# First tile of the combined projection: modulation weights split into a scale half and a shift half, the shift half loaded and used later

## The chip, the cores and the metric

One core of a Trainium2 chip. The metric is the device time of one execution in microseconds (us); the number given for a kernel is the median of several runs. Five engines work side by side from their own queues of instructions: TensorE (PE; PEld is its weight load), VectorE (DVE), ScalarE (ACT), GpSimd (POOL) and SyncE (SP), which here issues nearly all DMAs. SBUF is the on-chip memory of 128 partitions, PSUM the accumulator with 8 banks of 512 fp32 columns.

## The reference

One layer of a diffusion backbone over 512 latent tokens and 256 context tokens of width 1024. What matters for the change is its beginning:

```
mod = silu(c) @ w_mod + b_mod                    # 6 x 1024 columns; the same for c_ctx
sh1, sc1, gt1, sh2, sc2, gt2 = split(mod, 6)
h_lat = rmsnorm(x, norm1_g) * (1 + sc1) + sh1    # h_ctx likewise from ctx, c_ctx
p_lat = h_lat @ w_in                             # one projection, its columns feed everything after
```

Behind it come a bidirectional state-space mixer, a windowed attention, two gates, an output projection, and a gated convolutional feed-forward stage with a final norm. Everything is fp32.

## The kernel before, in words

Activations lie transposed, channels on the partitions: the 1024 channels are eight tiles of 128, and a tile of the latents is 128 x 512. Products that need fp32 accuracy are made of three passes with operands split in a high and a low part: high times high, high times low, low times high.

The opening stage (the block under `with tc.tile_pool(name="spool"`, lines 304 to 540) computes the modulation, the normed input and, at the same time, the first five column blocks of the projection (the gates g 0 to 4). So as to start before the norm is known, the first four tiles (`NU = 4`) are multiplied by the scale only (`scaled`, L410), their products are scaled by the norm afterwards (`scale_banks`), and the shift enters through a small product of its own (`shifts`, L427). For each tile j there are these steps, named by a letter in the string `order` (L518):

- A (`mod_rows`, L367): 8 products (16 PE instructions at L374, fp32 in two passes) of silu(c) with two loads of modulation weights, 2j and 2j + 1; each load holds half of the input channels and, for them, 128 shift columns and 128 scale columns of the tile. Four groups of 32 partitions of the bank `pmod` collect the sums in columns 0 to 255. ScalarE copies them out (L376), and the tile's projection weights `w0_raw[j]` are split (L149 and L150; the first tile on VectorE, L153 and L154). From tile 3 on, A also issues the load of the next tile's w0.
- B (`mod_cols`, L382): two products (four instructions, L384) turn the rows into columns, into `pmod` columns 256 to 259; ScalarE makes of them the scale `a1` (L385, from 258 and 259) and the shift `s1` (L386, from 256 and 257). Below these two are called a(j) and s(j).
- H (`prep`): `ah` and `al`, the high and the low part of x times the scale (L413 on ScalarE, L414 on VectorE), for the later tiles the normed input itself.
- P (`products`, L417): P0:02 is tile 0 on the output blocks 0 and 1, three passes (L422), and so on.
- Z (`shifts`, L427, L431): the shift times the raw w0 into the bank `pbias`, for the first four tiles.

sq_0 to sq_3 sum the squares of x (L397 on ScalarE, L399 on VectorE), sum_l (L241, then `ms` on VectorE, L251, and a power on GpSimd) and put_l make the norm of them; `hold` and `keep` are filler products on a bank that nobody reads.

What sets the order: PE runs exactly in the order of the string (`tc.manual_schedule`). SP's queue holds the loads in the order in which they are written (lines 331 to 347, then those that the steps issue), each with a wait when its buffer isn't free yet; modulation weights share six buffers, w0 four. ScalarE's and VectorE's queues are put in order when the kernel is built, by the builder's own view of what is ready; the copies of L376 and the squares of L397 are pinned behind what stands ahead of them in the text on their engine (`keep_in_program_order`). The waits between engines are put in by the builder too.

The order of the loads before: cc, modulation weights 0 and 1, the identity, a part of the vectors, w0 of tile 0, x tile 0, weights 2 and 3, w0 1, x tile 1, weights 4 and 5, w0 2, then x in three loads of two tiles, weights 6 and 7, w0 3, the other vectors. A load of modulation weights or of two x tiles has 512 KB, one of w0 320 KB, one of an x tile 256 KB.

Of the kernel before, what the change touches and what calls it, by code (L numbers as in the profile page):

```python
# [9 lines left out]
F32 = mybir.dt.float32  # L10
F32R = mybir.dt.float32r
U8 = mybir.dt.uint8
AF = mybir.ActivationFunctionType
# [5 lines left out]
P = 128  # L19
# [3 lines left out]
KT = D // P  # L23
# [4 lines left out]
V_BMOD = 0  # L28
V_N1 = 48
# [15 lines left out]
def tile_hybrid_layer(  # L45
# [33 lines left out]
    V, S, G, T = nc.vector, nc.scalar, nc.gpsimd, nc.tensor  # L79
# [221 lines left out]
    NU, NG = 4, 5  # L301
    first = {}
    gates = []
    with tc.tile_pool(name="spool", bufs=1) as sp:
        xs_ = sp.tile([P, KT, L], F32, name="xsb")
        xc_ = sp.tile([P, KT, LC], F32, name="xcb")
        csil32 = sp.tile([P, KT, 32], F32, name="csil32")
        s32 = sp.tile([P, KT, 32], F32, name="s32")
        s1 = s32[:, :, 0:2]
        still = sp.tile([P, 256], F32R, name="still")  # L310
        sel2 = sp.tile([P, 2], F32, name="sel2")
# [3 lines left out]
        def load_mod(i):  # L315
            t = sp.tile([P, 4, 256], F32, tag="wm", name="wm", bufs=6)
            nc.sync.dma_start(t, wm1[i].rearrange("p (k c) -> p k c", k=4))
            return t

        def load_w0(j):  # L320
            r = sp.tile([P, 640], F32, tag="w0", name="w0", bufs=4)
            nc.sync.dma_start(r, w0[j])
            return r

        def load_x(k):
            nc.sync.dma_start(xs_[:, 2 * k : 2 * k + 2, :], xT[k].rearrange("p (k t) -> p k t", k=2))
# [2 lines left out]
            nc.sync.dma_start(xs_[:, k, :], xT[k // 2, :, k % 2 * L : k % 2 * L + L])  # L329

        nc.sync.dma_start(ccs, cc)
        mod_raw = {i: load_mod(i) for i in range(2)}
        nc.sync.dma_start(ident, ident_d)
        nc.sync.dma_start(vec[:, :V_N2], vecs[:, :V_N2])
        w0_raw = {0: load_w0(0)}
# [4 lines left out]
        mod_raw.update({i: load_mod(i) for i in (4, 5)})  # L340
        w0_raw[2] = load_w0(2)
        load_x(1)
        load_x(2)
        load_x(3)
        mod_raw.update({i: load_mod(i) for i in (6, 7)})
        w0_raw[3] = load_w0(3)
        nc.sync.dma_start(vec[:, V_N2:], vecs[:, V_N2:])
        G.memset(raw(still), 1.0)
        G.memset(csil32, 0.0)
# [14 lines left out]
        pmod, pbias = accb(), accb()  # L364
        pg = [misb() for _ in range(NG)]

        def mod_rows(j):  # L367

            for u in range(2):
                i = 2 * j + u  # L370
                w = mod_raw.pop(i) if i in mod_raw else load_mod(i)
                for k in range(4):
                    z = slice(32 * k, 32 * k + 32)
                    T.matmul(pmod[z, 0:256], csil32[:, 4 * u + k, :], w[:, k, :], start=u == 0, stop=u == 1)  # L374
            row = tmp("tm")[:, :256]
            tc.keep_in_program_order(S.copy(row, pmod[:, 0:256]))  # L376
            if j + 1 < KT and j + 1 not in w0_raw:
                w0_raw[j + 1] = load_w0(j + 1)
            W[j] = split_w(j)
            return row  # L380

        def mod_cols(j, row):  # L382
            for i in range(2):
# [33 lines left out]
        def products(j, w, h, gs=range(NG)):  # L417

            st, en = j == 0, j in (NU - 1, KT - 1)
            for a, b in ((0, 0), (0, 1), (1, 0)):  # L420
                for i in gs:
                    T.matmul(  # L422
                        pg[i], w[a][:, i * P : (i + 1) * P], h[b], start=st and a + b == 0, stop=en and a == 1,
                        skip_group_check=True,
                    )

        def shifts(j):  # L427

            for g in range(3):
                n = 256 if g < 2 else P  # L430
                T.matmul(  # L431
                    pbias[32 * g : 32 * g + 32, 0:n], s32[:, j, :], w0_raw[j][:, 256 * g : 256 * g + n],
                    start=j == 0, stop=j == NU - 1,
                )

        r, W, H = {}, {}, {}
# [16 lines left out]
        def hold(n):  # L453
            for _ in range(n):
                T.matmul(unread[:, :256], still[:, :P], still, start=True, stop=True)
# [21 lines left out]
        def load_next():  # L477
# [9 lines left out]
        rows = {}  # L487
# [10 lines left out]
            "sq_2": lambda: squares(xs_, ssq, L, range(2, 4)),  # L498
            "sq_3": lambda: squares(xs_, ssq, L, range(4, 8)),
            "hold": lambda: hold(18),  # L500
            "keep": lambda: hold(6),
            "sq_c": lambda: squares(xc_, cq, LC, range(4)),
            "sq_d": lambda: squares(xc_, cq, LC, range(4, 8)),
            "sum_l": lambda: sums("l", ssq, 4),
# [11 lines left out]


        order = """  # L518
            hold A0 keep B0 H0 sq_0 keep Z0 P0:02 A1 P0:23 B1 H1 sq_1 P0:35 A2 P1:02 B2 H2 sq_2 P1:25 Z1 P2:02 sq_3 A3 P2:23 B3 H3
            P2:35 sum_l Z2 P3:02 A4 put_l P3:23 B4 H4 P3:35 scale_a Z3 scale_b rows A5 half P4:02 B5 H5 cols P4:25 A6  # L520
            P5:02 B6 H6 P5:24 A7 ctx N0 P5:45 B7 H7 next P6:02 N1 P6:25 N2 P7:02 sq_c N3 P7:25 sq_d
        """
        with tc.manual_schedule(engines={mybir.EngineType.PE}):
# [1563 lines left out]
def pack(  # L2087
    x, c, ctx, c_ctx, w_mod, b_mod, norm1_g, norm2_g, w_in, ssd_conv_w, ssd_conv_b, ssd_dt_bias, ssd_a_log, ssd_d,
    ssd_norm_g, w_o_ssd, w_o_att, att_sink, w_out, w_up, ffn_conv_w, ffn_conv_b, w_down, final_g,
):  # L2090
    f = lambda a: np.asarray(a)
    x, c, ctx, c_ctx, w_mod, w_in = f(x), f(c), f(ctx), f(c_ctx), f(w_mod)[0], f(w_in)[0]
    w_o_ssd, w_o_att, w_out, w_up, w_down = f(w_o_ssd)[0], f(w_o_att)[0], f(w_out)[0], f(w_up)[0], f(w_down)[0]
    ca = np.ascontiguousarray
    z0, xbc0, dt0 = 0, 2048, 5120
    q0 = dt0 + 64
    k0, v0, g0 = q0 + 1024, q0 + 1280, q0 + 1536
    half = np.r_[0:16, 32:48, 16:32, 48:64]
    perm = lambda base, heads: np.concatenate([base + 64 * h + half for h in range(heads)])
    A = np.arange  # L2100
    d = {}
    d["xT"] = ca(x[0].T.reshape(4, 2, P, L).transpose(0, 2, 1, 3).reshape(4, P, 2 * L))
    d["ctxT"] = ca(ctx[0].T.reshape(2, 4, P, LC).transpose(0, 2, 1, 3).reshape(2, P, 4 * LC))
    d["cc"] = ca(np.stack([c[0], c_ctx], 1).reshape(KT, P, 2).transpose(1, 0, 2))
    cw, fw = f(ssd_conv_w)[0], f(ffn_conv_w)[0]
    d["vecs"] = ca(
        np.concatenate(
            [_per_channel(f(a)) for a in (b_mod[0], norm1_g[0], norm2_g[0], final_g, ssd_norm_g[0])]
            + [_per_channel(cw[i]) for i in range(3)]
            + [_per_channel(f(ssd_conv_b)[0])]  # L2110
            + [_per_channel(fw[i]) for i in range(3)]
            + [_per_channel(f(ffn_conv_b)[0])],
            axis=1,
        )
    )
    dta = np.stack([f(ssd_dt_bias)[0].reshape(64), f(ssd_a_log)[0].reshape(64)], 1).reshape(2, 1, 32, 2)
    d["dta"] = ca(np.repeat(dta, 2, axis=1).reshape(P, 2))
    d["bc"] = ca(np.concatenate([f(ssd_d)[0], f(att_sink)[0]]))
    d["wm1"] = ca(w_mod[:, :2048].reshape(2, 4, P, 2, KT, P).transpose(4, 0, 2, 1, 3, 5).reshape(16, P, 1024))
    d["wm2"] = ca(w_mod[:, 2048:].reshape(4, 2, P, 8, 512).transpose(3, 0, 2, 1, 4).reshape(8, 4, P, 1024))  # L2120
    d["wq"] = _cols(w_in, perm(q0, 16))
    d["wk"] = _cols(w_in, perm(k0, 4))
    vdt = ca(w_in[:, np.r_[v0:g0, dt0:q0]].reshape(KT, P, 320).transpose(1, 0, 2)).reshape(P, KT * 320)
    d["wv"] = ca(np.pad(vdt, ((0, 0), (0, 320))).reshape(P, 3, 960).transpose(1, 0, 2))
    d["w0"] = ca(w_in[:, g0 : g0 + 640].reshape(KT, P, 640))
    d["wx"] = _cols(w_in, A(xbc0, dt0))
    d["wz"] = _cols(w_in, A(z0, xbc0))
    d["wg"] = _cols(w_in, A(g0, g0 + 2048))
    d["woa"] = _cols(w_o_att, A(1024))
    d["wos"] = _cols(w_o_ssd, A(1024))  # L2130
    d["wout"] = _cols(w_out, A(1024))
# [30 lines left out]
```

## Time and profile before

| | us |
|---|---|
| median of 3 runs | 1232.68 (1231.74 to 1234.01) |
| the profiled execution | 1232.22 |
| its span, first to last instruction | 1230.4 |
| PE busy | 1218.5 (99%) |
| VectorE busy | 914.1 (74%) |
| ScalarE busy | 687.0 (56%) |

A row of the timeline gives the start and the length of an instruction (or of several merged ones, xN), its engine, line and operation, out<-in, and in brackets how long the engine was idle ahead of it and what ended that. Matmuls are pipelined: a row of two has the length to the end of the second, and the next row can start before it ends. A row of the view by stretches gives start and end, then for PE, PEld, DVE, ACT and POOL the busy time and the number of instructions, then TensorE's granted clock, the share of the DMA engines' time that was used, and GB/s. A row of the DMA issues gives the transfer, its size and the time from issue to landing; where such a row is shown, it is of a window that holds that one issue. Buffers of `wm1` are called wm, those of `w0` w, those of x xsb.

### The profile page before, as it was taken

To read this page: it belongs to the slowest core of one execution; us is meant where nothing else is said; L and a number is where in the kernel's file an instruction comes from. 1 tells how busy PE (TensorE), PEld (TensorE's weight loads), DVE (VectorE), ACT (ScalarE), POOL (GpSimd) and SP (SyncE) were. 2 spreads that over 40 slices of the span, in tenths; PEclk is the share of its full clock that TensorE was granted. 3 is DMA by queue.
4 is the path that set the end of the run, shared out by engine and by line. 5 is a ranking of instruction groups with operands and counts; after the bars stand their busy time and mean duration, and the time that the engine had idled before them with its cause. 6 is when DMAs were issued, how large, how long until landed. Compare 5 with 4: busy or idle time off the path is not lost.

```text
span 1230.4 us, 17460 instructions
## 1 busy us (share of the span) xinstructions
PE 1218.5 (99%) x6328; PEld 996.3 (81%) x6328; DVE 914.1 (74%) x1484; ACT 687.0 (56%) x1302; POOL 167.9 (14%) x174
## 2 busy tenths in 40 slices
PE   9999999999999999999999999999999999999997
PEld 6798888888878877777777778888988888888886
DVE  4757888888555698697886786677688788886566
ACT  4657787787443556566586572223544444444543
POOL 0000111121100033333351530000200000000000
PEclk9999999999999999999999999999999999999999
DMA  9652678877946235345347466776144444457785
GB/s 354 245 159 89 218 194 194 212 198 211 225 141 211 91 123 147 121 131 185 122 138 203 136 205 221 225 245 236 48 166 148 145 150 153 153 169 248 243 318 183
DMA packets 108630, 224.65 MB, mean 183 GB/s; under 512 B 9600, under 2 KB 48832, under 8 KB 108544
## 3 DMA queue, kind: packets, MB, share of 16 engines
q1 hardware_dynamic: 101056, 197.32, 48.9%
q0 software_dynamic: 6912, 25.17, 8.7%
q8 instruction: 50, 0.82, 0.3%
q10 hardware_dynamic: 576, 1.05, 0.2%
q14 instruction: 36, 0.29, 0.1%
HBM read 193.29 MB, written 49.87 MB: 198 GB/s over the span
## 4 chain that ended last, share of the span: by engine, by line
PE 92%; DVE 3%; DMA 2%; ACT 2%; issue 1%; SPq 0%; POOLq 0%; ACTq 0%; DVEq 0%
PE acc L197 19%; PE acc L200 19%; PE acc L198 19%; PE acc L1919 3%; PE acc L1917 3%; PE acc L1918 3%; PE score L811 3%; PE po L860 3%; PE pt L847 2%; PE mis L1480 2%; PE mis L1385 2%; DMA wm<-wm 1%; PE mis L422 1%; PE acc L930 1%; PE acc L931 1%; PE acc L932 1%
## 5 line engine op out<-in xcount | busy, mean ns | idle before, releaser
L197 PE MATMUL acc<-hlh,whi 128*128 128x512 f32 x488 | 199.3, 408 | 0.0
L150 DVE TENSOR_TENSOR wlo<-wraw,whi 128x1024 fp32r<-128x1024 f32 (+2 forms) x119 | 143.4, 1207 | 71.9 <-ACT whi L149 62.2
L149 ACT CAST whi<-wraw 128x1024 fp32r<-128x1024 f32 (+2 forms) x119 | 122.8, 1033 | 127.4 <-PE acc L198 75.0
L200 PE MATMUL acc<-hlh,wlo 128*128 128x512 f32 x488 | 191.4, 392 | 0.0
L198 PE MATMUL acc<-hll,whi 128*128 128x512 f32 x488 | 190.7, 391 | 0.0
L197 PE MATMUL acc<-mh,whi 128*128 128x512 f32 x360 | 141.0, 392 | 0.0
L200 PE MATMUL acc<-mh,wlo 128*128 128x512 f32 x360 | 140.1, 389 | 0.0
L198 PE MATMUL acc<-ml,whi 128*128 128x512 f32 x360 | 140.0, 389 | 0.0
L200 PEld LDWEIGHTS acc<-hlh,wlo 128*128 128x128 f32 x488 | 91.6, 188 | 20.3
L198 PEld LDWEIGHTS acc<-hll,whi 128*128 128x128 f32 x488 | 91.9, 188 | 17.5 <-issue 1.7
L197 PEld LDWEIGHTS acc<-hlh,whi 128*128 128x128 f32 x488 | 91.8, 188 | 17.5 <-issue 2.2
L198 PEld LDWEIGHTS acc<-ml,whi 128*128 128x128 f32 x360 | 67.6, 188 | 14.5 <-issue 0.5
L197 PEld LDWEIGHTS acc<-mh,whi 128*128 128x128 f32 x360 | 67.6, 188 | 14.3 <-issue 0.5
L200 PEld LDWEIGHTS acc<-mh,wlo 128*128 128x128 f32 x360 | 67.6, 188 | 14.2
L820 DVE CUSTOM_DVE_ANT_0 p<-score,winm,nsink 128x512 f32<-128x512 f32 (+1 forms) x64 | 51.9, 810 | 15.2 <-PE score L811 13.7
L1268 DVE SCALAR_TENSOR_TENSOR ta<-acc,half,ta 128x511 f32<-128x511 f32 (+1 forms) x66 | 43.8, 663 | 25.7 <-ACT ta L1267 25.6
L1267 ACT ACTIVATE ta<-acc,half 128x512 f32<-128x512 f32 (+1 forms) x66 | 46.7, 708 | 27.0 <-PE acc L200 25.7
L1275 ACT ACTIVATE tb<-ta 128x512 f32<-128x512 f32 (+1 forms) x44 | 23.5, 534 | 65.2 <-DVE ta L1269 59.2
L827 ACT ACTIVATE p<-p,mneg 128x512 f32<-128x512 f32 (+1 forms) x64 | 49.7, 777 | 15.3 <-DVE mneg L820 14.7
L1387 POOL TENSOR_TENSOR st<-st,eT 128x512 f32<-128x512 f32 x24 | 33.5, 1396 | 170.5 <-ACT st L1405 162.3
L197 PE MATMUL acc<-hch,whi 128*128 128x256 f32 x176 | 54.4, 309 | 0.0
L855 DVE TENSOR_TENSOR ptl<-pt,pth 128x512 fp32r<-128x512 f32 x72 | 47.5, 686 | 8.5 <-ACT pth L851 7.8
(503 smaller groups left out, 2970.1 us busy)
## 6 DMA issues: line engine op xcount, KB each, us to landing
wraw<-wup SPq DMA_DIRECT2D x44, 512.0 KB, 3.6
wt_d<-wdn POOLq DMA_DIRECT2D x36, 512.0 KB, 7.8
fb<-cs_d SPq DMA_DIRECT2D x32, 512.0 KB, 6.6
wraw<-wm SPq DMA_DIRECT2D x32, 512.0 KB, 4.1
wraw<-wx SPq DMA_DIRECT2D x24, 512.0 KB, 3.5
wraw<-wt_d SPq DMA_DIRECT2D x20, 512.0 KB, 4.0
sp_d<-te SPq DMA_DIRECT2D x33, 256.0 KB, 2.1
wm<-wm SPq DMA_DIRECT2D x16, 512.0 KB, 7.7
```

The source lines that it names most:

```text
L149: S.copy(hi[:, :n], r[:, :n])
L150: V.tensor_tensor(lo[:, :n], r[:, :n], raw(hi[:, :n]), ALU.subtract)
L197: T.matmul(ps, wh, xh[:, k0 + k, :], start=a, stop=False)
L198: T.matmul(ps, wh, xl[:, k0 + k, :], start=False, stop=False)
L200: T.matmul(ps, wl, xh[:, k0 + k, :], start=False, stop=b)
L811: T.matmul(ps[:, o : o + len(z) * P], Q[h][:, b * P : (b + 1) * P], k[:, j, z[0] * P : (z[-1] + 1) * P], start=v == 0 and o % 512 in (0, P ...
L820: V.tensor_tensor_reduce(p[:, :w], d["ps"][i][:, o0 : o0 + w], m, op0=ALU.add, op1=ALU.min, scale=1.0, scalar=nsink[:, h : h + 1], accum_o ...
L827: S.activation(p, p, AF.Exp, bias=d["mneg"][:, i : i + 1], scale=-1.0, accum_out=d["den"][:, i : i + 1])
L855: V.tensor_tensor(d["ptl"][x], d["pt"][x], raw(d["pth"][x]), ALU.subtract)
L860: T.matmul(d["po"], vst[:, cols[x], j, :], d[y][x], start=x == 0 and y == "pth", stop=x == c - 1 and y == "ptl")
L1267: S.activation(o[:, :n], ps[:, :n], AF.Identity, scale=hcol(base_w, stride + i), bias=hcol(base_b, i))
L1268: V.scalar_tensor_tensor(o[:, 1:n], ps[:, 0 : n - 1], hcol(base_w, i), o[:, 1:n], ALU.mult, ALU.add)
```

## The change

The modulation weights of tile 0 are laid out another way on the host: load 0 holds all 1024 input channels for the 128 scale columns, load 1 the same for the 128 shift columns. (Those of the other tiles stay as they were.) A0 and B0 give way to four steps: S0 and a0 make the scale from load 0 alone, T0 and s0 the shift from load 1. S0's products go to `pmod` columns 0 to 127 and a0's to 258 and 259; T0's to columns 384 to 511, s0's to 256 and 257. Load 1 leaves the head of SP's queue. Weights 6 and 7 and w0 3 go ahead of the last two x loads, and load 1 goes behind them, ahead of these two. T0 follows A3, s0 follows B3; Z0 moves from ahead of P0 to ahead of Z2, behind P2:35, and sum_l now stands behind Z2. sq_3 moves behind T0. Inside the products of tile 0 the second and the third pass change places. w0 gets six buffers, and the fillers are 18, 3 and 8 in place of 18, 6 and 6.

```diff
-            r = sp.tile([P, 640], F32, tag="w0", name="w0", bufs=4)
+            r = sp.tile([P, 640], F32, tag="w0", name="w0", bufs=6)
...
         nc.sync.dma_start(ccs, cc)
-        mod_raw = {i: load_mod(i) for i in range(2)}
+        mod_raw = {0: load_mod(0)}
...
         load_x(1)
+        mod_raw.update({i: load_mod(i) for i in (6, 7)})
+        w0_raw[3] = load_w0(3)
+        mod_raw[1] = load_mod(1)
         load_x(2)
         load_x(3)
-        mod_raw.update({i: load_mod(i) for i in (6, 7)})
-        w0_raw[3] = load_w0(3)
...
+        def first_rows(i):
+            w = mod_raw.pop(i).rearrange("p k c -> p (k c)")
+            z0 = 0 if i == 0 else 3 * P
+            for u in range(2):
+                for k in range(4):
+                    z, c = slice(32 * k, 32 * k + 32), P * (4 * u + k)
+                    T.matmul(
+                        pmod[z, z0 : z0 + P], csil32[:, 4 * u + k, :], w[:, c : c + P], start=u == 0, stop=u == 1,
+                    )
+            row = tmp("tc")[:, :P]
+            tc.keep_in_program_order(S.copy(row, pmod[:, z0 : z0 + P]))
+            if i == 0:
+                W[0] = split_w(0)
+            return row
+
+        def first_cols(i, row):
+            c = 258 if i == 0 else 256
+            T.matmul(pmod[:, c : c + 2], row, sel2, start=True, stop=True)
+            if i == 0:
+                S.activation(a1[:, 0, :], pmod[:, c : c + 2], AF.Identity, scale=col(V_N1, 0), bias=bp1[:, 0:1])
+            else:
+                S.activation(s1[:, 0, :], pmod[:, c : c + 2], AF.Identity, bias=col(V_BMOD, 0))
...
-            for a, b in ((0, 0), (0, 1), (1, 0)):
+            for a, b in ((0, 0), (0, 1), (1, 0)) if j else ((0, 0), (1, 0), (0, 1)):
...
-                    start=j == 0, stop=j == NU - 1,
+                    start=j == 1, stop=j == NU - 1,
...
-            hold A0 keep B0 H0 sq_0 keep Z0 P0:02 A1 P0:23 B1 H1 sq_1 P0:35 A2 P1:02 B2 H2 sq_2 P1:25 Z1 P2:02 sq_3 A3 P2:23 B3 H3
-            P2:35 sum_l Z2 P3:02 A4 put_l P3:23 B4 H4 P3:35 scale_a Z3 scale_b rows A5 half P4:02 B5 H5 cols P4:25 A6
+            hold S0 keep_a a0 H0 sq_0 keep_b P0:02 A1 P0:23 B1 H1 sq_1 P0:35 A2 P1:02 B2 H2 sq_2 P1:25 Z1 P2:02 A3 T0 sq_3 P2:23 B3 s0 H3
+            P2:35 Z0 Z2 sum_l P3:02 A4 put_l P3:23 B4 H4 P3:35 scale_a Z3 scale_b rows A5 half P4:02 B5 H5 cols P4:25 A6
```

More of the change, by code (lines that the diff above doesn't have):

```diff
@@ L500, in tile_hybrid_layer @@
             "hold": lambda: hold(18),
-            "keep": lambda: hold(6),
+            "keep_a": lambda: hold(3),
+            "keep_b": lambda: hold(8),
+            "S0": lambda: rows.update(s=first_rows(0)),
+            "T0": lambda: rows.update(t=first_rows(1)),
+            "a0": lambda: first_cols(0, rows.pop("s")),
+            "s0": lambda: first_cols(1, rows.pop("t")),
             "sq_c": lambda: squares(xc_, cq, LC, range(4)),
@@ L2118, in pack @@
     d["bc"] = ca(np.concatenate([f(ssd_d)[0], f(att_sink)[0]]))
-    d["wm1"] = ca(w_mod[:, :2048].reshape(2, 4, P, 2, KT, P).transpose(4, 0, 2, 1, 3, 5).reshape(16, P, 1024))
+    wm = w_mod[:, :2048].reshape(2, 4, P, 2, KT, P)
+    d["wm1"] = ca(wm.transpose(4, 0, 2, 1, 3, 5).reshape(16, P, 1024))
+    for i in range(2):
+        d["wm1"][i] = wm[:, :, :, 1 - i, 0].transpose(2, 0, 1, 3).reshape(P, 1024)
     d["wm2"] = ca(w_mod[:, 2048:].reshape(4, 2, P, 8, 512).transpose(3, 0, 2, 1, 4).reshape(8, 4, P, 1024))
```

## The prediction, made before the change was run

> **What bounds the kernel now.** I read the page first, then the chain that ended last in order of time, then the busy times by stretch, and at last the timeline of the first 35 us instruction by instruction, with the time to landing of single transfers from the view of DMA issues.
>
> ```profile
> span 1230.4 us, 17460 instructions
> PE 92%; DVE 3%; DMA 2%; ACT 2%; issue 1%; SPq 0%; POOLq 0%; ACTq 0%; DVEq 0%
> ...
> 6.47 6.84 DMA xsb<-xT
> 13.37 10.55 DMA wm<-wm
> ...
> 10.00:24.00 14.00, 13.57 (x96) 8.44 (x95) 7.37 (x12) 8.57 (x19) 0.00 (x0) 1.00 1.03 415
> 28.60:57.00 28.40, 28.13 (x182) 19.93 (x181) 22.86 (x37) 17.21 (x40) 1.27 (x1) 1.00 0.64 240
> ```
>
> TensorE (PE) carries 92% of the chain. Of the 2% that are DMA most lies in the first 24 us, where the chain runs through x and the modulation weights: between 10 and 24 us the DMA engines are full (share 1.03, 415 GB/s), so 512 KB (524,288 B) cost 1.26 us of the stream. But PE is busy 13.57 of those 14 us as well. From 28.6 us on PE is busy 28.13 of 28.40 us. The change rewrites only what comes before P3:02, the first products of the fourth tile, at 28.62 us; the order behind it is the same, so whatever P3:02 gains or loses I carry to the end of the span. The ledger below is kept at that point.
>
> **The first x tile lands earlier.**
>
> ```profile
> 3.54 0.43 SPq L329 DMA_DIRECT2D xsb<-xT  x1
> ...
> xsb<-xT SPq DMA_DIRECT2D x1, 256.0 KB, 5.8
> ...
> 9.45 0.72 ACT L413 ACTIVATE ah<-xsb,a 128x512 fp32r<-128x512 f32 x1 [0.18 <-DMA xsb<-xT]
> 10.23 0.73 PE L422 MATMUL mis<-ah,w0h 128*128 128x512 f32 x2
> 11.02 0.73 PE L422 MATMUL mis<-al,w0h 128*128 128x512 f32 x2
> 12.14 1.07 PE L374 MATMUL acc<-wm,csil 128*32 128x256 f32 x16
> 13.14 0.50 PE L422 MATMUL mis<-ah,w0h 128*128 128x512 f32 x1
> ```
>
> The tile lands at 3.54 + 5.8 = 9.3 us, ScalarE waits for it, and P0 starts right behind. With the shift half of 512 KB out of the way it lands 1.26 us earlier, and w0_0 with it: **-1.26**. S0, half as wide as A0, fits ahead of it, since A0's second half waits for a transfer that no longer exists; and Z0 leaves this place. Both cost nothing here, because PE waits for x anyway; the eight filler products of keep_b lie in the same gap. The next line is the new order inside P0. One product takes 0.50 and two take 0.73, so the pitch is 0.23 to 0.24 and a pair takes 0.47; but the second pair follows the first by 0.79: a wait of 0.32 for al. w0l is ready before al once the weights come first, so putting it second ends this: **-0.32**.
>
> ```profile
> 6.84 1.22 SPq L317 DMA_DIRECT2D wm<-wm  x2
> ...
> wm<-wm SPq DMA_DIRECT2D x1, 512.0 KB, 8.2
> ...
> 15.87 1.07 PE L374 MATMUL acc<-wm,csil 128*32 128x256 f32 x16
> 22.53 0.63 PE L422 MATMUL mis<-ah,w0l 128*128 128x512 f32 x2
> 23.09 0.64 PE L374 MATMUL acc<-wm,csil 128*32 128x256 f32 x8
> 23.97 0.64 PE L374 MATMUL acc<-wm,csil 128*32 128x256 f32 x8 [0.24 <-DMA wm<-wm]
> 24.54 0.50 PE L422 MATMUL mis<-ah,w0h 128*128 128x512 f32 x1
> ```
>
> The second weights of A2 land at about 7.6 + 8.2 = 15.8 us, and A2 starts at 15.87. After the change they land at 14.5 and PE gets there at 15.87 - 1.58 = 14.3; the first eight products use the other transfer, 0.5 us long, so nothing is lost (0 to 0.3 the other way). At A3 PE would be free at 22.53 + 0.47 = 23.0 and done after 1.0 (12.14 to 13.14, a whole A), at 24.0; it is done at 24.54, because wm7 lands at 23.97. Now wm6 and wm7 go ahead of two x loads and the shift half, 1,536 KB or 3.8 us earlier: **-0.54**. These three make -2.12, so A3 ends at 24.54 - 2.12 = 22.42. The shift half then lands at 23.97 - 1,024 KB + 320 KB of w0_3, so -1.7, at 22.2: in time. That it takes the buffer of wm2 costs nothing either; A1 has read it by 11.6 (13.21 - 1.58), before SP comes to that issue, twelve transfers behind the first x tile. The two buffers more for w0 free SP from waiting on Z1, but no A behind A3 waits for weights (PE is full there): 0.
>
> **What is added to a full PE.** T0, s0 and Z0 all come in where PE has no gaps.
>
> ```profile
> 7.55 0.37 ACT L376 COPY tm<-acc 128x256 f32<-128x256 f32 x1 [4.96 <-PE acc L374]
> 8.11 0.53 PEld L384 LDWEIGHTS acc<-sel,tm 128*128 128x128 f32 x4
> 12.14 0.59 PEld L374 LDWEIGHTS acc<-wm,csil 128*32 128x32 f32 x16 [0.36 <-issue]
> 24.68 0.37 ACT L376 COPY tm<-acc 128x256 f32<-128x256 f32 x1 [1.54 <-PE acc L374]
> 25.34 0.50 PE L384 MATMUL acc<-sel,tm 128*128 128x2 f32 x4
> 25.71 0.71 PE L422 MATMUL mis<-ah,w0h 128*128 128x512 f32 x2
> 25.89 0.35 ACT L385 ACTIVATE a<-acc,bp,vec 128x2 f32<-128x2 f32 x1 [0.21 <-PE acc L384]
> 26.14 0.25 ACT L386 ACTIVATE s<-acc,vec 128x2 f32<-128x2 f32 x1
> ```
>
> T0 has as many instructions as an A (16), each half as wide. It lies between their weight loads alone, 0.59, and the 1.0 of an A; I take 0.65, near the loads, since the streaming halves. It writes columns 384 to 511 of the bank whose columns 0 to 255 ScalarE is copying out for A3. If PE must leave that bank alone, T0 waits: the copy ends at 24.68 + 0.37 = 25.05 on the old clock, and from a copy's end to the load that waits for it go 0.19 us (7.92 to 8.11), so 25.24 instead of 24.54, about 0.72 with the load. Bounds 0 and 0.72; I take 0.72, because in the kernel before A2's first product already waits on L386 of the tile ahead, which reads other columns of the same bank. No row of the trace shows that wait, as ScalarE is long done there. So T0: **+1.37**.
>
> The Trainium skill (PSUM — Partial Sum Buffer, section on bank collisions) speaks against the place: it says to guard by bank and quadrant and not by address, so separate columns do not help. By that rule T0 costs the 1.37; without it 0.65, and the whole sum would be 0.72 lower. No run so far shows it.
>
> s0 writes columns 256 and 257, which L386 of B3 reads. So it waits until a(3) and s(3) are through, and behind s0 on PE stand P2:35, Z0, Z2, sum_l and P3. On the old clock B3 ends at 25.84, a(3) starts at 25.89 and s(3) ends at 26.39; 0.19 later s0 can load, and its two instructions take 0.17 (four in 0.34), with 0.1 to the next product: P2:35 at 26.85 instead of 25.71, **+1.1** if ScalarE is free for a(3). That is the smallest price; the upper bound is in the first rival.
>
> ```profile
> 28.06 0.63 PE L431 MATMUL acc<-w,s 128*32 128x256 f32 x6
> 28.17 0.16 DVE L251 TENSOR_SCALAR ms<-acc 128x4 f32<-128x4 f32 x1 [1.64 <-PE acc L241]
> 28.25 0.74 DVE L414 SCALAR_TENSOR_TENSOR al<-xsb,a,ah 128x512 fp32r<-128x512 f32 x1
> 28.62 0.73 PE L422 MATMUL mis<-ah,w0h 128*128 128x512 f32 x2
> ```
>
> Z0 costs what Z2 does, 28.06 to 28.62: **+0.56**. Z2 now stands ahead of sum_l. Before, it covered VectorE's step ms, which waits for sum_l, and al(3) queued behind ms. If that queue keeps its order, al(3) ends some 1.0 us after P3:02 starts and its second pair waits 0.55; if al(3) goes first, 0. I take 0, as al(3) has its input a microsecond before sum_l ends.
>
> Sum: -1.26 - 0.32 - 0.54 + 1.37 + 1.1 + 0.56 = **+0.9 us**. The profiled execution took 1232.22 us with its span of 1230.4; the median of the three runs is 1232.68. The forecast is 1233.1 for the first and 1233.6 for the median. 0.2% (2.5 us, and the three runs lie 0.18% apart) is what can be told from no change; the forecast is well inside.
>
> **The rivals.** All turn on ScalarE's queue between T0 and Z0.
>
> ```profile
> 20.43 0.62 ACT L397 ACTIVATE tb<-xsb 128x512 f32<-128x512 f32 x1
> 20.95 0.61 ACT L397 ACTIVATE ta<-xsb 128x512 f32<-128x512 f32 x1
> ...
> 26.93 0.73 ACT L149 CAST w0h<-w 128x640 fp32r<-128x640 f32 x1
> 31.32 0.37 ACT L376 COPY tm<-acc 128x256 f32<-128x256 f32 x1 [3.67 <-PE acc L374]
> ```
>
> (A) *The squares stay ahead of a(3).* In the text the four squares of sq_3 come before B3. They used to run beside P2; now they follow T0's copy. On the new clock A3 ends at 22.42 and T0 1.37 later at about 23.8; its copy, half as wide as one of 0.37, is through at about 24.05 (an estimate). Four squares at a pitch of 0.52 (20.43 to 20.95) end at 26.15, and only then a(3), s(3), s0. On that clock the forecast has a(3) at 25.1, between the second and the third square, so this adds 1.05: +1.95, 1234.6. For it: the written order. Against: the order on ScalarE isn't the written one; the cast of the fifth tile's weights at 26.93 stands in the text behind the copy at 31.32.
>
> ```profile
> 9.39 0.33 SPq L326 DMA_DIRECT2D xsb<-xT  x1
> 10.66 0.33 SPq L326 DMA_DIRECT2D xsb<-xT  x1
> ...
> xsb<-xT SPq DMA_DIRECT2D x1, 512.0 KB, 8.5
> ...
> xsb<-xT SPq DMA_DIRECT2D x1, 512.0 KB, 9.7
> ```
>
> (B) *The last x load holds PE, and the kernel is slower.* By bytes it now lands where w0_3 did, at 23.97 + 0.79 = 24.8. In order A the third square is due at 25.1; every microsecond of landing past that goes through squares, a(3), s(3) and s0 to PE. It is slower by over 0.2% from a landing at 25.6 on. Once in this trace a load came 1.2 us later than its bytes: the second of the x(1) to x(3) loads landed at 20.4, the one ahead at 17.9. At 26.0: 0.9 more than A, +2.85, 1235.5.
>
> (C) *T0 runs beside the copy*, the bank being no obstacle: +0.2, 1232.9. If s0's wait is covered too, -0.9: 1231.8. More than the 2.12 us of waits that are removed cannot be won here, so a gain over 2.5 us needs something outside this stage.
>
> (D) *The first x tile does not come earlier*, because the start of the queue, not its bytes, sets the landing: SP's issues are 0.43 apart. Then +2.2, 1234.8. Against it: the tile lands 5.8 us after its issue, so most of that time is spent behind other transfers.
>
> (E) The builder's order on ScalarE and VectorE shifts elsewhere; the row at 26.93 shows that it does such things. Either sign, up to 3 us.
>
> **How the numbers follow.** Forecast 0.38, A 0.20, B 0.12, C 0.14, D 0.06, E 0.10. Slower by over 0.2%: B, a tail of A and D of 0.02, and 0.03 of E, 0.17. Faster: 0.08, nearly all of it E. Within: 0.75. The range runs from 1231.5, a little under C's better end for what E may add, to 1235.6, just past B.
>
> **What would show it.** P0's first product near 8.97 us; A3 done near 22.4; a gap of 0.7 us on PE ahead of T0, ended by ScalarE's copy; a gap of 0.7 to 2 us ahead of s0 ended by L386; in the queue of ScalarE the place of a(3) among the squares; P3:02 at 29.5, and the end of the span 0.9 us later. I am wrong if P3:02 starts before 28.6, if T0 follows A3 without a gap, or if the shift at P3:02 is not the shift at the end.

## The result: slower by 0.25%, and a stretch of TensorE at half clock

Over 15 runs each the changed kernel takes 1234.81 us (1233.69 to 1240.37) and the kernel before 1232.56 us (1231.74 to 1234.01) in the median; the ratio is 1.0025, with a 95% interval of 1.0017 to 1.0033. The forecast was 1233.6, with a difference inside 0.2% as the likeliest case; the measured 0.25% lies just past that, and its interval reaches down to 0.17%. The sign of the sum was right, the size too small. The profiled execution took 1235.31 us, its span 1233.5 us.

Of the page of the changed kernel, the span and the shares of the chain that ended last:

```profile
span 1233.5 us, 17495 instructions
PE 91%; DMA 3%; DVE 2%; ACT 1%; issue 1%; SPq 0%; POOL 0%; POOLq 0%; ACTq 0%; DVEq 0%
```

From its view by stretches, the same 14 us as before and two stretches of 3.4 us (start and end, length, busy time of PE, PEld, DVE, ACT and POOL, granted clock, DMA share, GB/s):

```profile
10.00:24.00 14.00, 13.35 (x111) 8.38 (x111) 5.88 (x8) 7.16 (x16) 0.00 (x0) 1.00 1.03 416
22.84:26.26 3.42, 1.87 (x23) 1.46 (x23) 0.54 (x1) 1.72 (x7) 0.00 (x0) 1.00 1.04 420
26.26:29.67 3.41, 3.26 (x8) 2.25 (x8) 2.92 (x6) 2.62 (x6) 0.00 (x0) 0.50 1.02 415
```

The span is 3.1 us longer; the chain has 3% of DMA instead of 2. The first 24 us look alike: the DMA engines are as full (416 GB/s to 415), PE a little less busy (13.35 us to 13.57). Then PE is busy for only 1.87 us of the stretch from 22.84 to 26.26, and in the one behind it, for all of its 3.41 us, TensorE's granted clock is 0.50. The kernel before has no such stretch ahead of its last 10 us, in which both kernels show one; "half clock" below means ahead of those. The timeline of the changed kernel shows where it lies:

```profile
8.37 0.72 PE L447 MATMUL mis<-ah,w0h 128*128 128x512 f32 x2 [0.40 <-ACT ah L438]
9.95 1.07 PE L375 MATMUL acc<-wm,csil 128*32 128x256 f32 x16
13.23 1.55 SPq L326 DMA_DIRECT2D xsb<-xT  x2
14.48 0.64 PE L375 MATMUL acc<-wm,csil 128*32 128x256 f32 x8 [0.16 <-DMA wm<-wm]
21.34 1.07 PE L375 MATMUL acc<-wm,csil 128*32 128x256 f32 x16
22.48 0.37 ACT L377 COPY tm<-acc 128x256 f32<-128x256 f32 x1 [0.73 <-PE acc L375]
22.90 0.64 PE L390 MATMUL acc<-wm,csil 128*32 128x128 f32 x16 [0.49 <-ACT tm L377]
23.48 0.50 PE L447 MATMUL mis<-ah,w0h 128*128 128x512 f32 x1
23.61 0.27 ACT L394 COPY tc<-acc 128x128 f32<-128x128 f32 x1 [0.76 <-PE acc L390]
24.82 0.35 ACT L410 ACTIVATE a<-acc,bp,vec 128x2 f32<-128x2 f32 x1 [0.93 <-PE acc L409]
25.07 0.62 ACT L422 ACTIVATE ta<-xsb 128x512 f32<-128x512 f32 x1
25.59 0.62 ACT L422 ACTIVATE tb<-xsb 128x512 f32<-128x512 f32 x1
26.11 0.25 ACT L411 ACTIVATE s<-acc,vec 128x2 f32<-128x2 f32 x1
26.41 0.59 PE L401 MATMUL acc<-sel,tc 128*128 128x2 f32 x2 [1.63 <-ACT s L411]
26.86 1.20 PE L447 MATMUL mis<-ah,w0h 128*128 128x512 f32 x2
29.70 1.06 PE L456 MATMUL acc<-w,s 128*32 128x256 f32 x12
30.68 1.05 PE L241 MATMUL acc<-rmsc,ssq 128*128 128x1 f32 x8
31.60 0.70 PE L447 MATMUL mis<-ah,w0h 128*128 128x512 f32 x2
```

Among the DMA issues from 11.5 to 14.6 us the last two x loads stand in one row, with the median of their times to landing (10.2 and 10.3):

```profile
xsb<-xT SPq DMA_DIRECT2D x2, 512.0 KB, 10.2
```

(L375 is A, L377 its copy, L390 T0, L394 T0's copy, L401 s0, L410 a(j), L411 s(j), L422 the squares, L447 the products, L456 Z.) P0 starts at 8.37 instead of 10.23, and A3 runs whole, without a wait for wm7. T0 waits until ScalarE has copied A3's sums. Then a(3) starts at 24.82, but two squares stand between it and s(3), so s0 waits 1.63 us. Behind s0, P2:35 takes 26.86 to 29.70, 2.84 us where the kernel before needs 1.47, from 25.71 to the start of its sum_l:

```profile
27.18 0.94 PE L241 MATMUL acc<-rmsc,ssq 128*128 128x1 f32 x8
```

P3:02 starts at 31.60 instead of 28.62: +2.98. The span is longer by nearly the same, 3.1 us.

The squares could have run sooner. x(2) landed at 13.23 + 10.2 = 23.4, and behind T0's copy (23.61, 0.27 us long) ScalarE stood idle for 0.93 us ahead of a(3).

### The profile page after: what moved, and what is told of

Read it like the earlier page. It is cut to its first block, busy times and chain, and to the rows that moved or that the text cites. A ratio compares the mean times of both kernels' runs of the same rounds, so it can differ in the third digit from the quotient of the medians.

```text
span 1233.5 us, 17495 instructions
## 1 busy us (share of the span) xinstructions
PE 1219.2 (99%) x6343; PEld 997.9 (81%) x6343; DVE 914.9 (74%) x1484; ACT 686.9 (56%) x1303; POOL 167.5 (14%) x174
## 3 DMA queue, kind: packets, MB, share of 16 engines
q10 hardware_dynamic: 576, 1.05, 0.2%
## 4 chain that ended last, share of the span: by engine, by line
PE 91%; DMA 3%; DVE 2%; ACT 1%; issue 1%; SPq 0%; POOL 0%; POOLq 0%; ACTq 0%; DVEq 0%
PE acc L197 20%; PE acc L200 20%; PE acc L198 20%; PE score L841 3%; PE po L890 3%; PE pt L877 2%; PE mis L1510 2%; PE mis L1415 2%; PE mis L447 2%; PE acc L1947 1%; PE acc L1948 1%; PE acc L1949 1%; PE mis L1516 1%; PE acc L960 1%; PE acc L962 1%; PE acc L961 1%
## 5 line engine op out<-in xcount | busy, mean ns | idle before, releaser
L198 PEld LDWEIGHTS acc<-ml,whi 128*128 128x128 f32 x360 | 67.6, 188 | 14.6 <-issue 0.5
L850 DVE CUSTOM_DVE_ANT_0 p<-score,winm,nsink 128x512 f32<-128x512 f32 (+1 forms) x64 | 51.9, 811 | 15.1 <-PE score L841 13.6
```

Of the source, the lines that this page charges most:

```text
L198: T.matmul(ps, wh, xl[:, k0 + k, :], start=False, stop=False)
L850: V.tensor_tensor_reduce(p[:, :w], d["ps"][i][:, o0 : o0 + w], m, op0=ALU.add, op1=ALU.min, scale=1.0, scalar=nsink[:, h : h + 1], accum_o ...
```

## The experiments

The first four ran beside a kernel before of 1232.04 us, the second four beside one of 1232.18, the last four beside one of 1232.37. At first I had two theories: (1) the added instructions make waits where they stand, in the bank and in ScalarE's order, and the thin stretch of PE that they leave halves the clock; (2) the last two x loads are simply too late, and the squares and sum_l with them.

**T0 and s0 in a bank that nobody reads.** The filler products' bank takes the place of `pmod` for both steps.

```diff
-                        pmod[z, z0 : z0 + P], csil32[:, 4 * u + k, :], w[:, c : c + P], start=u == 0, stop=u == 1,
+                        (unread if i else pmod)[z, z0 : z0 + P], csil32[:, 4 * u + k, :], w[:, c : c + P], start=u == 0, stop=u == 1,
...
```

> T0 and s0 write the bank of the fillers instead of pmod; nothing else changes. Theory 1 (s0 waits for s(3), which stands behind two squares, and the thin stretch that this makes halves the clock): T0 follows A3 without the 0.56 us gap, s0 goes ahead of s(3), P2:35 starts near 24.2 us at full clock; the next thing late is sum_l, which waits for the last squares until about 28.4, so P3:02 at about 29.4 instead of 31.6 and the time 2.2 us under the changed kernel, 1232.6. Theory 2 (the x loads that were moved back hold the squares, and PE's own waits are only where this shows): P3:02 stays within 0.5 us of 31.6, time 1234.5 or so.

Measured: 1236.75 us (1234.38 to 1238.65), ratio 1.0036 [1.0024, 1.0049]. PE in the timeline of this run:

```profile
22.06 1.07 PE L375 MATMUL acc<-wm,csil 128*32 128x256 f32 x16
22.95 0.62 PE L390 MATMUL acc<-wm,csil 128*32 128x128 f32 x16
24.67 0.36 PE L401 MATMUL acc<-sel,tc 128*128 128x2 f32 x2
29.65 1.02 PE L241 MATMUL acc<-rmsc,ssq 128*128 128x1 f32 x8 [2.00 <-DVE ssq L424]
```

Both waits are gone: T0 follows A3 without a gap and s0 stands right behind B3. So both were waits on `pmod`, as the prediction had it. T0's was for the bank: T0 writes columns 384 to 511, the copy that it waits for reads 0 to 255. For s0 the run doesn't tell the bank from the columns, as s0 writes 256 and 257, the very columns that s(3) reads. But sum_l now waits 2.00 us for the last square, and a stretch of half clock comes from 31.5 to 34.9. The wait was moved, not removed. P3:02 is at 30.54, between the two theories, and the time above what either gave.

**The four squares behind s0.**

```diff
-A3 T0 sq_3 P2:23 B3 s0 H3
+A3 T0 P2:23 B3 s0 sq_3 H3
```

> The squares of the last four x tiles move behind s0 in the text; a(3), s(3) and s0 now come ahead of them on ScalarE. Theory 1: s0's wait falls from 1.6 to about 0.75 us, P2:35 starts near 25.8; if 0.75 is too short to halve the clock it takes 1.5 us, otherwise 2.8. Either way the squares end later and sum_l waits for them until about 29.6, P3:02 at about 30.5, time 1.1 us under the changed kernel, 1233.7. Theory 2: squares that start a microsecond later make it a microsecond worse, P3:02 near 32.5, time 1235.8.

Measured: 1235.6 us (1235.19 to 1238.16), 1.0032 [1.0020, 1.0045]. Of its timeline:

```profile
26.04 0.38 PE L401 MATMUL acc<-sel,tc 128*128 128x2 f32 x2 [0.60 <-ACT s L411]
30.54 1.02 PE L241 MATMUL acc<-rmsc,ssq 128*128 128x1 f32 x8 [1.64 <-DVE ssq L424]
```

s0's wait falls from 1.63 to 0.60 and no half clock follows, not even behind the 1.64 us at sum_l; the squares come too late for sum_l instead, by 1.64. P3:02 is at 31.42, again between the two theories, and the time near the 1235.8 of theory 2. ScalarE has to get s(3) early and the squares early.

**Filler products ahead of s0**, thirteen of them, so that PE isn't idle there.

```diff
-A3 T0 sq_3 P2:23 B3 s0 H3
+A3 T0 sq_3 P2:23 B3 keep_c s0 H3
...
+            "keep_c": lambda: hold(13),
```

> Thirteen filler products on the unread bank between B3 and s0, some 1.6 us of PE work that ends when s(3) does; queues of the other engines as in the changed kernel. Theory 1 (the clock was halved for lack of work): s0 starts at 26.4 as before, but P2:35 takes 1.5 us in place of 2.8 and the granted clock stays 1.00 from 26 to 30 us; P3:02 at about 30.2, time 1.4 us under the changed kernel, 1233.4, and the runs lie closer together. If P2:35 was slow for its operands or the DMA traffic, or under theory 2: no change, P2:35 2.8 us, P3:02 at 31.6, time 1234.8.

Measured: 1236.9 us (1235.38 to 1238.34), 1.0039 [1.0027, 1.0052]. The first x tile landed at 10.0 in this profile, PE waited 2.87 us for it, and the half clock came there, from 11.7 to 15.1. At the place in question P2:35 takes 1.57 us (30.24 to 31.81) at full clock, as theory 1 said for this place. The 1233.4 that it gave for the time did not come. In the profiled execution, the longest of the five (1238.34), the late tile covers any gain; what kept the other four at 1235.4 to 1237.9 no profile shows.

**The bank change with the norm later**: sq_3 behind H3, sum_l behind P3:02, put_l behind P3:23.

```diff
-A3 T0 sq_3 P2:23 B3 s0 H3
-P2:35 Z0 Z2 sum_l P3:02 A4 put_l P3:23 B4 H4
+A3 T0 P2:23 B3 s0 H3 sq_3
+P2:35 Z0 Z2 P3:02 sum_l A4 P3:23 put_l B4 H4
```

> As e1_bank, and the squares behind H3, sum_l behind P3:02 and put_l behind P3:23, so that PE never waits for the squares. Theory 1: P3:02 at about 26.8, P3:35 at about 32.0 against 32.7 before the change; the norm in SBUF at about 32.0 against 32.5, so the end 0.5 us ahead of the kernel before, 1232.1, and 2.7 under the changed one. Theory 2: the norm comes out 1 us or more later than in the kernel before, because its last input lands at 24.8 instead of 21.5; time over 1233.6.

Measured: 1240.77 us (1237.17 to 1242.13), 1.0073 [1.0059, 1.0087], the worst of all. P3:02 starts at 26.09, but 40 us further down PE waits, as its row shows:

```profile
72.42 0.50 PE L197 MATMUL acc<-hlh,whi 128*128 128x512 f32 x1 [1.85 <-ACT whi L149]
```

Here a cast of weights comes late from ScalarE, and half clock follows from 73.4 to 76.8. Both expectations stopped at the norm and missed it. The profile is of the fastest of the five executions (1237.17); the 3.6 us from it to the median it can't show.

**Fillers in every gap**: 20 instead of 8 ahead of P0, 4 ahead of T0, 13 ahead of s0.

```diff
-            "keep_b": lambda: hold(8),
+            "keep_b": lambda: hold(20),
+            "keep_t": lambda: hold(4),
+            "keep_c": lambda: hold(13),
```

> The changed kernel with filler products of one more kind of place: 20 instead of 8 ahead of P0, 4 new ones between A3 and T0 and 13 new ones between B3 and s0. They write a bank that nobody reads and fill gaps in which TensorE waits anyway; ScalarE's and VectorE's orders stay those of the changed kernel. Theory 1 (the thin stretch ahead of s0 halves TensorE's clock for the next 3.4 us, which makes P2:35 take 2.84 us where 1.47 are its price): no stretch of half clock before 55 us, P2:35 back to about 1.5 us, P3:02 about 1.4 us earlier against P0 than in the changed kernel's profile (21.9 us from P0's start instead of 23.2), the time about 1233.4, and the spread of the runs narrower. Theory 2 (the waits alone make the loss and the clock is only read off beside them): P0 to P3:02 stays at 23.2 us or grows by fillers that run past the wait, and the time is 1234.8 or more. If the fillers run past the waits by 0.2 to 0.5 us, theory 1 gives 1233.6 to 1233.9.

Measured: 1236.3 us (1234.88 to 1237.34), 1.0031 [1.0019, 1.0042]. In the profile there is no half clock, P2:35 takes 1.57 us and P0 to P3:02 21.51 us instead of 23.23. The expected 1233.4 did not come. Part of that is an error of mine: the first tile landed at 7.4 there, and the 20 fillers ran until 9.18, so P0 started 0.8 us later than in the changed kernel. The rest, among it the 1.4 us from the profiled execution (1234.88) to the median, it doesn't show.

**The loads alone**: the kernel before with wm6, wm7 and w0_3 ahead of x(2) and x(3), six buffers for w0 (not among the lines below), and sq_3 behind A3.

```diff
-        load_x(2)
-        load_x(3)
         mod_raw.update({i: load_mod(i) for i in (6, 7)})
         w0_raw[3] = load_w0(3)
+        load_x(2)
+        load_x(3)
...
-P2:02 sq_3 A3 P2:23 B3 H3
+P2:02 A3 sq_3 P2:23 B3 H3
```

> The kernel before with only the loads moved: wm6, wm7 and w0_3 ahead of x(2) and x(3), six buffers for w0, and the squares of sq_3 behind A3 in the text. The first tile's weights are not split; A0, B0 and Z0 stand where they stood. Theory 1 (the loss comes from the instructions put between A3 and P3:02): about the time before, within 0.5 us (1231.6 to 1232.6), A3 without its wait for wm7 (0.5 us earlier) and at most that much given back at sum_l. Theory 2 (the loss comes from the x tiles that land later, through the squares to sum_l and P3:02): sum_l waits 1.5 us or more for the squares, P3:02 is 1 us or more later, and the time is 1233.2 or more.

Measured: 1237.45 us (1236.61 to 1237.81), 1.0039 [1.0026, 1.0053]. No T0, no s0, and yet no less is lost than by the change (its interval overlaps that of the change). ScalarE's rows in its timeline, then PE's at sum_l:

```profile
25.51 0.72 ACT L413 ACTIVATE ah<-xsb,a 128x512 fp32r<-128x512 f32 x1
26.13 0.62 ACT L397 ACTIVATE ta<-xsb 128x512 f32<-128x512 f32 x1
...
30.17 1.02 PE L241 MATMUL acc<-rmsc,ssq 128*128 128x1 f32 x8 [3.59 <-DVE ssq L399]
```

sum_l waits 3.59 us, and half clock follows (31.7 to 35.1). Theory 1 as I had put it falls: T0 and s0 aren't needed for the loss. But x(2) had landed at 23.0 and x(3) at 24.3; it is the place behind ah(3) that starts the first of the four squares at 26.13. So a third theory: the place that the squares get on ScalarE, once the x loads are late, decides.

**The split with the old order of the loads**, the shift half last, sq_3 ahead of A3 again, T0 behind P2:35, s0 behind sum_l, Z0 behind P3:02. Of the edit, the second line of the order:

```diff
-P2:35 Z0 Z2 sum_l P3:02 A4
+P2:35 T0 sum_l s0 Z2 P3:02 Z0 A4
```

> The split of the first tile's weights is kept, but the added products stand where nothing should have to wait: T0 behind P2:35 and s0 behind sum_l, Z0 behind P3:02; x(2) and x(3) go back ahead of wm6, wm7 and w0_3, and the shift half is loaded last, so A3 waits for wm7 as before. Theory 1 (the loss is the waits of T0 and s0 in the bank, the place of the squares and the halved clock): the work added is 0.6 + 0.2 + 0.56 = 1.4 us, the head gains 1.3 to 1.9, no gap over 0.5 us on TensorE between A3 and P3:02 and no half clock: -0.5 to +0.2 against the time before, 1231.5 to 1232.3. Theory 2 (late x loads, then squares): the same here, since x is early again; so it tells how much of the loss is place and how much is the split itself. If the split costs in itself (something in S0, or in the x tile's landing), P0 is later than 9 us and the time 1233.5 or more.

Measured: 1233.02 us (1231.40 to 1234.91), 1.0002 [0.9994, 1.0011]: no difference. P3:02 starts at 28.74, 0.12 behind the kernel before, with Z0 (0.56) still to come; no half clock. Here the split costs about what it brings.

**The same with only x(3) behind wm6, wm7 and w0_3**, sq_3 in two pairs, one ahead of A3 and one behind H3.

> As the run with the split late, but wm6, wm7 and w0_3 go ahead of x(3) and the shift half behind it is still last; two of sq_3's squares stand ahead of A3 and two behind H3. Theory 1: A3 loses its wait for wm7 (0.5 us better), sum_l has its squares in time if x(3) lands by 24.5: -0.4 to -1.0 against the time before, 1231.0 to 1231.6. Theory 2 (a single x load landing late is enough): sum_l waits 0.5 us or more for the squares and the gain at A3 is given back there: 1231.6 to 1232.4.

Measured: 1236.4 us (1233.74 to 1237.89), 1.0027 [1.0016, 1.0038], 4 us above what either theory gave; neither counted on the clock. PE at sum_l, at P3:02 and at the spread step of the norm:

```profile
26.94 1.02 PE L241 MATMUL acc<-rmsc,ssq 128*128 128x1 f32 x8 [1.41 <-DVE ssq L424]
28.67 0.74 PE L447 MATMUL mis<-ah,w0h 128*128 128x512 f32 x2
33.28 0.65 PE L258 MATMUL acc<-ident,rs 128*128 128x128 f32 x4
```

The last two of these places in the run above:

```profile
28.74 0.73 PE L447 MATMUL mis<-ah,w0h 128*128 128x512 f32 x2
31.75 0.65 PE L258 MATMUL acc<-ident,rs 128*128 128x128 f32 x4
```

and the stretches ahead of the half clock and in it:

```profile
26.01:29.43 3.42, 2.49 (x19) 2.01 (x20) 1.37 (x4) 0.88 (x2) 1.02 (x1) 1.00 1.03 418
29.43:32.84 3.41, 3.41 (x24) 1.78 (x25) 0.53 (x1) 0.00 (x0) 0.00 (x0) 0.52 1.02 412
```

P3:02 is 0.07 earlier than in the run above, and its span is 1.5 us longer (1232.9 to 1231.4). The spread step of the norm (L258), the same work behind P3:02 in both, starts 4.61 us behind it here and 3.01 there. That is the price of one stretch at half clock, measured at nearly equal starts: about 1.6 us.

**The changed kernel once more.**

> The changed kernel once more, unchanged, beside the experiments, with a second profile. If its runs are alike from one occasion to the next: 1234.8 again (ratio 1.0025 to the kernel before), P0 between 8.2 and 10.9 us with the first x tile's landing (7.3 to 10.0 in the profiles so far), P0 to P3:02 23.2 us if one 3.4 us stretch of half clock follows s0 and 21.8 if not. If the variants so far (1235.6 to 1236.9 for the ones that take a wait out of it) were measured in worse conditions than the changed kernel was: 1236 to 1237 here, and their ratios must be read against this one.

Measured: 1236.21 us (1234.26 to 1238.63), 1.0035 [1.0023, 1.0047], an interval that overlaps the first one. So the variants above at 1.0031 to 1.0039 cannot be told from the changed kernel. The timeline of its second profile:

```profile
26.05 0.38 PE L401 MATMUL acc<-sel,tc 128*128 128x2 f32 x2 [1.63 <-ACT s L411]
26.29 0.70 PE L447 MATMUL mis<-ah,w0h 128*128 128x512 f32 x2
27.86 1.06 PE L456 MATMUL acc<-w,s 128*32 128x256 f32 x12
29.95 0.71 PE L447 MATMUL mis<-ah,w0h 128*128 128x512 f32 x2
```

and two stretches that lie to s0 as those of the first profile do:

```profile
22.48:25.90 3.42, 1.88 (x23) 1.46 (x23) 0.54 (x1) 1.72 (x7) 0.00 (x0) 1.00 1.04 421
25.90:29.31 3.41, 3.11 (x23) 2.03 (x23) 3.31 (x7) 2.51 (x6) 0.00 (x0) 1.00 1.02 416
```

The wait at s0 is the same 1.63 and the stretch ahead as thin (1.88 to 1.87), but the clock stays at 1.00 and P2:35 takes 1.57 us (26.29 to 27.86). P3:02 is at 29.95, +1.33, and the span at 1232.4. The wait is the kernel's, the half clock comes in some executions only. So the full clock at s0 with fillers, seen in one profile of each of the two runs, doesn't show that the fillers kept it.

**The squares of x(2) between A3's copy and T0's copy, those of x(3) behind s0's step.** Nothing else is changed.

```diff
-            "sq_3": lambda: squares(xs_, ssq, L, range(4, 8)),
+            "sq_3": lambda: squares(xs_, ssq, L, range(4, 6)),
+            "sq_4": lambda: squares(xs_, ssq, L, range(6, 8)),
...
-A3 T0 sq_3 P2:23 B3 s0 H3
+A3 sq_3 T0 P2:23 B3 s0 H3 sq_4
```

> The changed kernel with the four squares of sq_3 in two pairs: those of x(2) between A3's copy and T0's copy on ScalarE, those of x(3) behind s0's step, none between a(3) and s(3). Theory 1 (the place of the squares is what fails: ahead of s(3) they hold s0, behind ah(3) all four of them hold sum_l): s0 starts 0.5 us behind a(3) or less and no later than 25.7, sum_l waits less than 0.3 us, no stretch of half clock; P0 to P3:02 20.7 to 21.0 us, the ledger of the prediction: about +0.6 against the time before, 1232.8. Theory 2 (x(2) and x(3) land too late, whatever the place of the squares): sum_l still waits 1 us or more for the last square's add, P0 to P3:02 22 us or more, 1234.5 or more.

Measured: 1233.77 us (1233.15 to 1237.55), 1.0013 [1.0005, 1.0022], and a span of 1231.2. Its timeline:

```profile
22.88 0.63 ACT L422 ACTIVATE ta<-xsb 128x512 f32<-128x512 f32 x1
23.41 0.62 ACT L422 ACTIVATE tb<-xsb 128x512 f32<-128x512 f32 x1
24.90 0.35 ACT L410 ACTIVATE a<-acc,bp,vec 128x2 f32<-128x2 f32 x1 [0.72 <-PE acc L409]
25.15 0.25 ACT L411 ACTIVATE s<-acc,vec 128x2 f32<-128x2 f32 x1
25.46 0.38 PE L401 MATMUL acc<-sel,tc 128*128 128x2 f32 x2 [0.60 <-ACT s L411]
25.70 0.71 PE L447 MATMUL mis<-ah,w0h 128*128 128x512 f32 x2
28.36 1.02 PE L241 MATMUL acc<-rmsc,ssq 128*128 128x1 f32 x8
29.25 0.71 PE L447 MATMUL mis<-ah,w0h 128*128 128x512 f32 x2
```

s(3) follows a(3) at once, s0 waits 0.60, sum_l waits for nothing, no half clock, and P3:02 is at 29.25, +0.63. The loads, the bank, T0, s0 and Z0 are those of the changed kernel. So the place of four instructions of 0.62 us on an engine that isn't the bound makes the difference between this and the changed kernel: 2.4 us in the medians of the two runs side by side, and 1.04 us at s0 (2.01 to 0.97 in the table below) between the profiles with half clock in neither, whose spans differ by 1.2. The interval lies below that of the changed kernel's second occasion (from 1.0023) and overlaps that of its first (from 1.0017).

**The loads alone, the squares ahead of A3** as in the kernel before; otherwise the run of the loads alone.

> The kernel before with only the loads moved, as in the run that took 1237.45, but with the four squares left where the kernel before has them, ahead of A3's copy on ScalarE. Theory 1 (place of the squares): A3's copy waits for the last square (x(3) lands at 24.3, so the copy at 25.4 instead of 23.9) and B3 with it, 1.3 us, less the 0.8 us by which A3 ends earlier: P3:02 at about 29.1 instead of 28.62, sum_l without a wait for the squares, 1232.7; a stretch of half clock behind the gap would add 1.4. Theory 2 (late x whatever the place): sum_l waits 1.5 us or more, P3:02 at 30.5 or later, 1235 or more.

Measured: 1238.71 us (1237.07 to 1242.02), 1.0055 [1.0043, 1.0067]. From PE and ScalarE:

```profile
28.77 0.73 PE L422 MATMUL mis<-ah,w0h 128*128 128x512 f32 x2
...
66.95 3.60 ACT L616 ACTIVATE ta<-acc 32x512 f32<-32x512 f32 x6
...
70.57 1.04 ACT L149 CAST whi<-wraw 128x1024 fp32r<-128x1024 f32 x1
...
71.67 0.50 PE L197 MATMUL acc<-hlh,whi 128*128 128x512 f32 x1 [1.85 <-ACT whi L149]
```

At P3:02 it is as the place theory says, and better: 28.77 (+0.15, where 29.1 was expected), 2.9 us earlier than with the squares behind ah(3), sum_l without a wait. The late x loads cost nearly nothing there. The total is another matter: at 71.67 PE waits for the same late cast as in the run with the norm later. In the kernel before ScalarE starts this cast at 67.40; here the builder has put it behind six copies (L616, 3.60 us together), at 70.57. The whole order on ScalarE is made anew for every text, and this one has a hole 40 us further down. PE's product that waits for `E` (L1486) starts at 544.03 instead of 541.28, +2.75; the 1.8 us by which the span (1234.9) grows beyond that come behind it and were not traced.

**The split late with Z2 and s0 ahead of sum_l**, in the 1.41 us where PE waited, and four fillers behind them.

```diff
-P2:35 T0 sum_l s0 Z2 P3:02 Z0 A4
+P2:35 T0 Z2 s0 keep_c sum_l P3:02 Z0 A4
```

> The run with the split late and wm6, wm7, w0_3 ahead of x(3), with Z2 and s0 moved ahead of sum_l into the 1.4 us in which TensorE waited for the last square, and four fillers behind them. Theory 1: sum_l keeps its start at about 26.9 us, no stretch of half clock follows (there was one at 29.4 to 32.8, worth 1.5 us), P3:02 at 27.9 to 28.1 instead of 28.67: with Z0 behind it, -0.3 to -0.8 against the time before, 1231.4 to 1231.9. Theory 2 (x(3)'s landing alone sets sum_l, and varies from run to run): sum_l later than 27.5 in the profile, 1233 or more with a spread of 3 us.

Measured: 1232.62 us (1231.54 to 1234.88), 1.0005 [0.9997, 1.0014]. The mechanism came as expected: sum_l at 26.76 without a wait, P3:02 at 27.65, no half clock, a span of 1230.2. The time cannot be told from the kernel before. It was the attempt at a version that beats both, and it does not.

## Why the prediction was wrong, step by step

| step | forecast | changed kernel | second profile | squares moved |
|---|---|---|---|---|
| up to A3's end (24.54 before) | -2.12 | -2.20 | -2.56 | -2.12 |
| T0 with its wait | +1.37 | +1.14 | +1.13 | +1.14 |
| s0 with its wait | +1.10 | +2.21 | +2.01 | +0.97 |
| P2:35 itself | 0 | +1.37 | +0.10 | +0.08 |
| Z0, sum_l | +0.56 | +0.46 | +0.65 | +0.56 |
| P3:02 (28.62 before) | +0.9 | +2.98 | +1.33 | +0.63 |

Each number is the difference of two starts in the timelines, against the same difference in the kernel before; where T0 waits behind A3, A3's end is its start plus 1.00, the length of a whole A (for s0: from P2:23 to P2:35, 23.48 to 26.86 against 24.54 to 25.71); "squares moved" is the run with sq_3 in two pairs and nothing else changed.

*Right.* The three terms of the head make -2.20 together, against -2.12, though in part by luck: P0 came 1.86 us earlier, more than the 1.26 of the bytes, A2 gave 0.37 back while waiting for its second weights, and A3 gained 0.45 instead of 0.54. T0 waited 0.56, the load counted, against 0.72, and worked 0.58 against 0.65. The bank rule cited from the Trainium skill (PSUM — Partial Sum Buffer, bank collisions) agrees with the trace at T0: its columns are not those that ScalarE's copy reads, it waits 0.49 all the same, and doesn't wait in another bank. s0's 1.63 say nothing on the rule, since s0 writes the columns that s(3) reads. Both are waits that the build put in; what the chip would do without them no run here shows. Z0 and al(3) were right too. The carry from P3:02 to the end came out (+2.98 to a span of +3.1), but with some luck: at the product that waits for `E` (L1516) the changed kernel is only 2.18 behind (543.46 to 541.28), and later PE waits 0.72 for a DMA at 1142.57, where the kernel before shows no wait. In the second profile +1.33 is 0.58 there and 2.0 in the span, with the squares moved +0.63 is -0.04 and 0.8. Elsewhere the carry held within some 0.8 us, apart from the two runs with the late cast and the three where half clock lies behind P3:02.

*The step that failed* is s0: "+1.1 if ScalarE is free for a(3). That is the smallest price". The smallest price was taken into the sum. ScalarE was indeed free for a(3), but not for s(3), since the builder put two of the four squares between the two. That is rival A in another place and at its price: 25.07 to 26.11 is 1.04, where A had 1.05. With the squares moved, s0 costs 0.97 and the whole ledger comes out at +0.63, the median at 1233.77, 1.4 above that of the kernel before beside it: the forecast was about that of a kernel with another order on ScalarE. The prediction had quoted the row that shows the builder changing that order, and still gave its favourable case the greater chance.

*What was missing* is the clock. No rival had it: a stretch where PE works for only 1.87 of 3.41 us, and then 3.41 us at half clock, +1.37 in P2:35. It adds to the wait ahead of it. It is not in every execution (the second profile has none), so it is a share of the difference in the median and not the whole of it.

The other rivals: the last x loads landed at 23.4 and about 24.7, as by their bytes, so B did not happen; T0 did not run beside the copy (C); the first tile did come earlier (D). The builder's order elsewhere (E) cost nothing visible in the changed kernel: the cast that starts at 67.40 in the kernel before starts at 70.37, +2.97. It is what cost time in the two runs with the late cast.

What stays open: the runs of the changed kernel spread over 6.7 us, those of the kernel before over 2.3. The three longest of the changed kernel's (1238.0 to 1240.4) have a mean granted clock of 0.993 to 0.994 instead of 0.996 to 0.998, which is more than one halved stretch (an estimate: 3.41 us at half clock in a span of 1233.5 take 0.0014 off the mean); where the others lie no profile caught. The filled variant, without half clock in its profile, was not faster in the median, and that isn't explained. So how much of the 2.25 us in the median is the wait at s0 and how much the clock stays open too.

## What to carry to other kernels

Before moving a load behind others, list the cheap instructions that read it on an engine that isn't the bound, and see on that engine's own queue what they will stand ahead of: two squares, 1.04 us together, between two small instructions that the bottleneck waits for cost nearly what a whole load of 512 KB out of the way was forecast to bring (1.26 us). Where a builder makes that order, read the order that it built, all of it, not only near the change. And take two profiles before a clock stretch is charged to an edit.

## What the runs showed of the hardware that was not expected

A stretch of half clock lasted 3.4 us each time, and cost 1.4 to 1.6 us here. In each of the six profiles that have one it came behind a stretch of 3.4 us in which PE was busy for only 0.81 to 2.49 us: 1.87 in the changed kernel, with no single gap over 1.7 us; but with 1.88 us in the second profile of the changed kernel it did not come, nor with 1.55 of 3.40 us around the late cast in the loads-alone run with the squares ahead (68.40 to 71.80). The Trainium skill (TensorE: Matmul & The Clock Gate, Part 1) speaks of a free-running activity window of about 3.4 us, and of falling back to half rate after a window of idle time. The length agrees. The trace differs in that PE need not be idle: half a window of work did not always keep the clock. A free-running window could explain why the same gap is followed by half clock in one execution and not in another, by how it falls on the window's edges; where no half clock comes, no run here shows those edges.

The first x tile, behind the same loads, landed between 7.3 and 8.3 us in the profiles of the split kernels, and once at 10.0. The kernel before would hide such a delay in part, since its A3 waits for weights anyway (0.54 us); no run here shows it.
